# Weight tiles in three pools instead of one: where the operands of TensorE lie modulo 256 bytes

## The chip, the cores and the metric

The kernel runs on one core of a Trainium2 chip. The metric is the device time of one execution in microseconds (us), the median of several runs. "ns" is marked where it is meant.

## What is computed

One layer of a streaming encoder for two groups of tokens that share weights: 256 positions of a new stream and 32 of a running one, 288 together, with d_model 2048. Cut to what matters:

```python
xn = rmsnorm(x, norm_mix_pre)
u, z, xbc, dt = split(xn @ w_in)                  # 2048 -> 1024 + 2048 + 2560 + 32
mix = concat[pool_mixer(u), ssd_mixer(z, xbc, dt)] @ w_out      # 3072 -> 2048
x = x + rmsnorm(mix, norm_mix_post)
up = causal_dwconv(rmsnorm(x, norm_ffn_pre) @ w_up)             # 2048 -> 2 x 5632
x = x + rmsnorm((silu(gate) * value) @ w_down, norm_ffn_post)   # 5632 -> 2048
```

All is float32 in and out. The four large products are nearly all of the work.

## The kernel before

**Three products for one.** [...] A product of weights W and tokens A is then W_hi x A_hi + W_hi x A_lo + W_lo x A_hi. `mm3` issues these as three matmuls, on lines 144, 145 and 146; below they are called a triple. Each has 128 x 128 weights and 288 columns of tokens, and each loads its own weights first (on the page the loads are PEld). Tokens (`xn`, `mixs` and `mixp`, `hn`, `fa`: the inputs of the four large products) are tiles of 128 x 2 x 288 float32: the high half in front, the low half 1152 bytes behind it.

**Weights.** `fetch_w` (L119) loads `raw`, 8 tiles of contraction by 256 outputs, 8192 bytes per partition; `split_w` (L126) makes from each half of it a `whi` (ScalarE copies and rounds, L138) and a `wlo` (VectorE subtracts, L139), 4 contraction tiles by 256 outputs, 4096 bytes per partition each. All three kinds come from the pool `wpool`, four buffers of each tag (`hi`, `lo`, `raw`). `project` (L148) runs such a product: it walks over the contraction in chunks of 8 tiles (`ksplit`), for each chunk over the parts of 4, in each part over the two groups of 128 outputs, and in each of these over the 4 contraction tiles, one triple each, into one accumulator per 128 outputs. In the output projection the chunks are (8, 8), (16, 8), (0, 8): the SSD channels first (`mixs`), then the pooled channels `mixp0` to `mixp7`.

**Other users of TensorE.** The first stage (L361) multiplies the first columns of w_in by `xn` with weight tiles `w` of its own (both parts in one tile, in the pool `xin`), while the input still arrives: it holds 288 matmuls of 288 columns, hi x A_hi, hi x A_lo, lo x A_hi for each contraction tile and output. Its loads go to `raw` tiles, with one contraction tile into slots of the tags `hi` and `lo`. `state_mm` (L974) makes the new states, 512 columns at a time, with weights `bt_h` and `bt_l`. The last projection works with L1265 (high weights times both halves of 160 columns), L1266 (low weights, 288 columns) and L1288 (roles turned). L267 are 12 matmuls on a constant tile `busy` that run before the input is there.

**Addresses.** A pool's tiles stand behind each other in each partition, at multiples of 32 bytes, and pools stand in the order in which they are opened: `const`, `wpool`, `side`, `apool` (token tiles), `bpool`, then the stage's own. `side` holds four small tiles (`hp`, `eps_t`, `warm`, `rec`: 32 + 32 + 32 + 64 = 160 bytes). Weight and token tiles, and the steps between the slices of them that matmuls read (512 and 1024 bytes for weights), are such that each kind starts at one residue modulo 256, whichever buffer it is in (2304 bytes between token tiles is 9 x 256).

The order of instructions comes from a scheduler (`tc.high_priority`, `tc.issue_after` and `pin` bind it in places); the built programs have been laid beside each other for what the change does to it.

Of the kernel before, what the change touches and what calls it, by code (L numbers as in the profile page):

```python
# [8 lines left out]
F32 = mybir.dt.float32  # L9
F32R = mybir.dt.float32r  # L10
# [6 lines left out]
P = 128  # L17
# [8 lines left out]
HEADS = 32  # L26
# [16 lines left out]
NB = 768  # L43
# [15 lines left out]
def body(  # L59
# [23 lines left out]
    act, dve, pool, pe, sp = nc.scalar, nc.vector, nc.gpsimd, nc.tensor, nc.sync  # L83

    const = ctx.enter_context(tc.tile_pool(name="const", bufs=1))
    wpool = ctx.enter_context(tc.tile_pool(name="wpool", bufs=4))
    side = ctx.enter_context(tc.tile_pool(name="side", bufs=1))
    apool = ctx.enter_context(tc.tile_pool(name="apool", bufs=16))
    bpool = ctx.enter_context(tc.tile_pool(name="bpool", bufs=20))
    acc_ps = ctx.enter_context(tc.tile_pool(name="acc_ps", bufs=5, space=PSUM))  # L90
# [26 lines left out]
    pin = tc.keep_in_program_order  # L117

    def fetch_w(view, kb, nk, c0, nc_):  # L119
        raw = wpool.tile([P, nk, nc_], F32, tag="raw", name="raw")  # L120
        with tc.high_priority(offset=ahead[0]):
            group, c = divmod(c0, 2 * P)
            sp.dma_start(out=raw, in_=view[group, :, kb : kb + nk, c : c + nc_])
        return raw

    def split_w(raw, kb, nk, nc_, after=()):  # L126

        out = []
        step = min(nk, 1024 // nc_)
        for k in range(0, nk, step):  # L130
            n = min(step, nk - k)
            hi = wpool.tile([P, n, nc_], F32R, tag="hi", name="whi")
            lo = wpool.tile([P, n, nc_], F32R, tag="lo", name="wlo")
            with ExitStack() as order:
                order.enter_context(tc.high_priority(offset=ahead[0]))
                for ins in after:
                    order.enter_context(tc.issue_after(ins.ins))
                act.activation(hi, raw[:, k : k + n, :], AF.Copy)  # L138
                dve.tensor_tensor(lo, raw[:, k : k + n, :], hi.bitcast(F32), op=ALU.subtract)  # L139
            out.append([(kb + k + i, hi[:, i, :], lo[:, i, :]) for i in range(n)])  # L140
        return out
# [6 lines left out]
    def project(view, groups, acts, ksplit, before=None, done=None, spare=(), hold=(), behind=None, wait=(), tail=()):  # L148


        n_all = sum(-(-w // P) for _, w in groups)
        accs = [acc_ps.tile([P, NT], F32, tag="acc", name="acc") for m in range(n_all - len(spare))]
        accs.extend(spare)
        k_first, k_last = ksplit[0][0], ksplit[-1][0] + ksplit[-1][1] - 1
        after = before(*ksplit[0]) if before else None
        for i, (kb, n) in enumerate(ksplit):
            raws = [fetch_w(view, kb, n, c0, w) for c0, w in groups]
            nxt = None
            if before and i + 1 < len(ksplit):
                nxt = before(*ksplit[i + 1])  # L160
            m0 = 0
            for raw, (c0, w) in zip(raws, groups):
                parts = split_w(raw, kb, n, w, tuple(wait) + ((after or ()) if m0 else ()) + (hold if i else tail if m0 + w // P == n_all else ()))
                for q, part in enumerate(parts):
                    for m in range(w // P):
                        c = slice(m * P, (m + 1) * P)
                        with ExitStack() as order:
                            if behind and part[-1][0] == k_last and m0 + m > SUMS_AFTER:
                                order.enter_context(tc.issue_after(behind[-1].ins))
                            for k, hi, lo in part:  # L170
                                mm3(accs[m0 + m], hi[:, c], lo[:, c], acts[k], k == k_first, k == k_last)
                        if done and i + 1 == len(ksplit) and q + 1 == len(parts):
                            done(m0 + m, accs[m0 + m])
                m0 += w // P
            after = nxt
        return accs
# [33 lines left out]
    def first_load(i):  # L210

        kb, n = CHUNKS[i]
        raw = wpool.tile([P, n, NB], F32, tag="raw" if n > 1 else ("hi", "lo")[i % 2], name="raw")
        for j, c in enumerate((slice(0, NB),) if i else PIECES):
            pin((sp if i or j == 2 else act).dma_start(out=raw[:, :, c], in_=w_first[:, kb : kb + n, c]))
        raws.append(raw)

    input_load(0, 1)
    first_load(0)
    for i, (k0, k1) in enumerate(zip(INPUT[:-1], INPUT[1:])):  # L220
        input_load(k0, k1, sp if i else act)
        for j in range(2 * i + 1, 2 * i + 3):
            first_load(j)
    w_dt = xin.tile([P, KD, HEADS], F32, name="w_dt")
    pin(sp.dma_start(out=w_dt, in_=w_dt_in))
    first_load(9)
    cols = const.tile([P, sum(n for _, n in COLS)], F32, name="cols")
    pin(sp.dma_start(out=cols, in_=cols_in))
    hp = side.tile([HEADS, 3], F32, name="hp")
    pin(sp.dma_start(out=hp, in_=heads_in))  # L230
    col = {}
    for name, n in COLS:
# [2 lines left out]

    ones = const.tile([P, P], F32, name="ones")
    pool.memset(ones, 1.0)
    eps_t = side.tile([P, 1], F32, name="eps_t")
    pool.memset(eps_t, EPS)
    warm = side.tile([P, 1], F32, name="warm")  # L240
    pin(act.activation(warm, eps_t, AF.Copy))
    ident = const.tile([P, P], F32, name="ident")
    make_identity(nc, ident)
# [1 line left out]
    pool.affine_select(  # L245
        out=tri, in_=ones, pattern=[[1, P]], compare_op=ALU.is_ge, fill=0.0, base=0, channel_multiplier=-1
    )
    rec = side.tile([P, 16], F32, name="rec")
    for t in range(16):
        pool.memset(rec[:, t : t + 1], 1.0 / (t + 1))  # L250
    scan_one = const.tile([HEADS, NT], F32, name="scan_one")
# [572 lines left out]
    def pool_group(i):  # L824
        raw = fetch_w(w_pool, 2 * i, 2, 0, 256)
        wq = split_w(raw, 0, 2, 256)[0]
        for j in range(2):
            o = aux([P, NT], "acc_x") if j else acc_ps.tile([P, NT], F32, tag="acc", name="acc")
            c = slice(j * P, (j + 1) * P)
            for k, hi, lo in wq:  # L830
                mm3(o, hi[:, c], lo[:, c], uin[2 * i + k], k == 0, k == 1)
            a = op_.tile([P, 2, NT], F32R, name=f"mixp{2 * i + j}")
            split_from(a, o, p_scale[:, 2 * i + j : 2 * i + j + 1])
            mix[2 * i + j] = a
# [199 lines left out]
    late = []  # L1034
# [189 lines left out]
    K22 = [(0, 8), (8, 8), (16, 6)]  # L1224
    C1, C0 = slice(P, NT), slice(0, P)
    raws = [fetch_w(w_down[:, :, HALF:, :], kb, n, A * P, 256) for kb, n in K22]
    parts = []
    for (kb, n), raw in zip(K22, raws):
        for k in range(0, n, 4):
            m = min(4, n - k)  # L1230
            if len(parts) < 4:
                hi = wpool.tile([P, m, 256], F32R, tag="hi", name="whi")
                lo = wpool.tile([P, m, 256], F32R, tag="lo", name="wlo")
            else:
                rest = wpool.tile([P, 2, 4, 256], F32R, tag="raw", name="wlast")
                hi, lo = rest[:, 0, :m], rest[:, 1, :m]
            act.activation(hi, raw[:, k : k + m, :], AF.Copy)
            dve.tensor_tensor(lo, raw[:, k : k + m, :], hi.bitcast(F32), op=ALU.subtract)
            parts.append([(kb + k + i, hi[:, i, :], lo[:, i, :]) for i in range(m)])
    late_ = wpool.tile([P, 6 * P], F32, tag="raw", name="late")  # L1240
    ft.append(late_[:, : 4 * P])
    g_row = late_[:, 4 * P :]
    sp.dma_start(out=g_row, in_=norm_ffn_post[:, A * P :].broadcast_to([P, 2 * P]))
# [160 lines left out]
```

## Time and profile before

| | |
|---|---|
| median of 3 runs | 1322.2 us (1322.06 to 1324.41) |
| the profiled execution | 1322.35 us |
| its span, first to last instruction | 1320.6 us |
| TensorE busy | 1313.9 us, 99% |
| VectorE, ScalarE, GpSimd busy | 894.7, 672.5, 251.8 us |
| granted TensorE clock, mean | 1.000 |

A row of the timeline has start and duration in us, engine, line, operation, the tiles that it writes and reads, and its shape. Starts of consecutive matmuls tell how fast TensorE runs; a matmul's duration (some 0.29 us for 288 columns) is longer than the distance to the next one, since they overlap. In the windows a row has a stretch, its length, each engine's busy time with the number of its instructions that touch the stretch, the granted clock, and the busy share of the DMA engines. In the groups, "busy, mean ns of one | idle time before" follows the name and the count.

### The profile page before, as it was taken

Reading aid. Unit: us, or ns where it says so; the run is one execution under the profiler, and the core shown is the slowest. Engines: PE = TensorE matmul, PEld = TensorE weight load, DVE = VectorE, ACT = ScalarE, POOL = GpSimd, SP = SyncE. Lnnn points to the kernel's source line nnn. Section 1 sums busy time; section 2 is a strip of 40 time slices with the busy share of each in tenths; the row PEclk is TensorE's granted clock in tenths of the full one; section 3 lists DMA queues with packets and bytes.
Section 4 is the critical chain, followed back from the end, with each engine's and each line's share of the span. In section 5 each row is a group of like instructions: output and inputs, shape, how many; then the busy total and the mean of one; then the engine's idle time right before and its main releaser. Section 6 shows DMA issues by size and latency. Waiting matters only on the chain.

```text
span 1320.6 us, 25268 instructions
## 1 busy us (share of the span) xinstructions
PE 1313.9 (99%) x10043; PEld 1302.5 (99%) x10043; DVE 894.7 (68%) x1515; ACT 672.5 (51%) x1013; POOL 251.8 (19%) x399
## 2 busy tenths in 40 slices
PE   9999999999999999999999999999999999999998
PEld 9999999999999999999999999999999999999997
DVE  7998988879655588867766744336666666755454
ACT  7557767446543567544444433334444444444442
POOL 2342222222232221211211200001111111201110
PEclk9999999999999999999999999999999999999999
DMA  8578875445566478666445454455544554466763
GB/s 336 190 217 269 290 220 177 156 163 207 199 218 218 141 197 269 197 179 206 164 160 165 160 166 173 157 171 177 175 160 161 174 173 165 160 228 187 212 178 114
DMA packets 110038, 251.75 MB, mean 191 GB/s; under 512 B 64736, under 2 KB 73856, under 8 KB 87392
## 3 DMA queue, kind: packets, MB, share of 16 engines
q1 hardware_dynamic: 103424, 233.22, 54.7%
q0 software_dynamic: 5824, 16.13, 4.1%
q8 instruction: 78, 1.28, 0.4%
q10 hardware_dynamic: 672, 0.80, 0.2%
q14 instruction: 40, 0.33, 0.1%
HBM read 237.11 MB, written 13.00 MB: 189 GB/s over the span
## 4 chain that ended last, share of the span: by engine, by line
PE 96%; DMA 1%; DVE 1%; ACT 1%; issue 0%; SPq 0%; ACTq 0%
PE acc L145 30%; PE acc L144 30%; PE acc L146 30%; DMA raw<-in_w_first 1%; PE py L633 1%; PE acc L1265 0%; DVE w L300 0%; PE acc L1266 0%; PE acc_t L1288 0%; PE acc_x L145 0%; PE acc_x L144 0%; PE acc_x L146 0%; DVE sq L320 0%; PE py L635 0%; PE acc L361 0%; PE acc_x L361 0%
## 5 line engine op out<-in xcount | busy, mean ns | idle before, releaser
L139 DVE TENSOR_TENSOR wlo<-raw,whi 128x1024 fp32r<-128x1024 f32 (+1 forms) x396 | 472.9, 1196 | 311.9 <-ACT whi L138 310.3
L138 ACT ACTIVATE whi<-raw 128x1024 fp32r<-128x1024 f32 (+1 forms) x396 | 408.4, 1033 | 475.8 <-PE acc L145 394.1
L146 PE MATMUL acc<-hn,wlo 128*128 128x288 f32 x1376 | 404.5, 295 | 0.0
L145 PE MATMUL acc<-hn,whi 128*128 128x288 f32 x1376 | 403.6, 294 | 0.0
L144 PE MATMUL acc<-hn,whi 128*128 128x288 f32 x1376 | 402.9, 294 | 0.5 <-ACT hn L1041 0.4
L144 PEld LDWEIGHTS acc<-hn,whi 128*128 128x128 f32 x1376 | 258.8, 189 | 1.4 <-ACT hn L1041 0.8
L145 PEld LDWEIGHTS acc<-hn,whi 128*128 128x128 f32 x1376 | 258.5, 188 | 0.1
L146 PEld LDWEIGHTS acc<-hn,wlo 128*128 128x128 f32 x1376 | 258.3, 188 | 0.0
L146 PE MATMUL acc<-fa,wlo 128*128 128x288 f32 x660 | 194.6, 295 | 0.0
L145 PE MATMUL acc<-fa,whi 128*128 128x288 f32 x660 | 194.2, 294 | 0.0
L144 PE MATMUL acc<-fa,whi 128*128 128x288 f32 x660 | 194.0, 294 | 0.0
L146 PE MATMUL acc<-xn,wlo 128*128 128x288 f32 x608 | 179.5, 296 | 0.0
L144 PE MATMUL acc<-xn,whi 128*128 128x288 f32 x608 | 179.4, 295 | 0.0
L145 PE MATMUL acc<-xn,whi 128*128 128x288 f32 x608 | 178.9, 294 | 0.0
L144 PEld LDWEIGHTS acc<-fa,whi 128*128 128x128 f32 x660 | 124.5, 189 | 0.0
L145 PEld LDWEIGHTS acc<-fa,whi 128*128 128x128 f32 x660 | 124.1, 188 | 0.0
L146 PEld LDWEIGHTS acc<-fa,wlo 128*128 128x128 f32 x660 | 123.9, 188 | 0.0
L1091 POOL COPY fc_stage<-ebuf 128x4 f32<-128x4 f32 x88 | 26.9, 306 | 476.8 <-DVE ebuf L1090 455.4
L144 PEld LDWEIGHTS acc<-xn,whi 128*128 128x128 f32 x608 | 114.6, 189 | 0.7 <-issue 0.5
L145 PEld LDWEIGHTS acc<-xn,whi 128*128 128x128 f32 x608 | 114.3, 188 | 0.0
L146 PEld LDWEIGHTS acc<-xn,wlo 128*128 128x128 f32 x608 | 114.2, 188 | 0.1
L1086 POOL COPY ebuf<-cols 128x2 f32<-128x2 f32 x88 | 74.0, 842 | 108.7 <-DVE fc L1097 61.2
(338 smaller groups left out, 1800.1 us busy)
## 6 DMA issues: line engine op xcount, KB each, us to landing
raw<-in_w_up SPq DMA_DIRECT2D x80, 1024.0 KB, 5.1
raw<-in_w_in SPq DMA_DIRECT2D x38, 1024.0 KB, 5.2
raw<-in_w_down SPq DMA_DIRECT2D x32, 1024.0 KB, 5.0
raw<-in_w_out SPq DMA_DIRECT2D x24, 1024.0 KB, 5.0
raw<-in_w_down SPq DMA_DIRECT2D x16, 768.0 KB, 4.4
raw<-in_w_up SPq DMA_DIRECT2D x14, 512.0 KB, 4.2
gb<-g_d POOLq DMA_DIRECT2D x8, 832.0 KB, 6.3
raw<-in_w_first SPq DMA_DIRECT2D x5, 768.0 KB, 12.8
```

The source lines that it names most:

```text
L138: act.activation(hi, raw[:, k : k + n, :], AF.Copy)
L139: dve.tensor_tensor(lo, raw[:, k : k + n, :], hi.bitcast(F32), op=ALU.subtract)
L144: then(pe.matmul(out, wh, a[:, 0, :], start=start, stop=False))
L145: then(pe.matmul(out, wh, a[:, 1, :], start=False, stop=False))
L146: then(pe.matmul(out, wl, a[:, 0, :], start=False, stop=stop))
L633: ins = pe.matmul(y[c, 0:256], xw[:, 0, f_], m[:, h, 0:256], start=True, stop=False)
L1086: pool.tensor_copy(e[:, 258:260], hist_f[:, :, i])
L1091: pool.tensor_copy(fc_stage[:, :, :, i], e[:, 256:324].rearrange("p (s c) -> p s c", c=34)[:, :, 0:2])
```

## The change

`wpool` becomes three pools, opened in the order high, (side1), low, raw. `side1` holds only `rec`, 64 bytes; the other three small tiles go into `const`, which grows by 96. So the high parts move by 96 bytes, the low and raw ones by 160, and the token pool stays where it was. Sizes and numbers of buffers are the same. Start addresses modulo 256 in the two built programs:

| | before | after |
|---|---|---|
| `whi` | 64 | 160 |
| `wlo` | 64 | 224 |
| `raw` (and `wlast`, the last two parts of w_down) | 64 | 224 |
| first-stage `raw` of one contraction tile, in slots of `hi` and `lo` | 64 | 160, 224 |
| `xn`, `mixs`, `hn`, `fa`, `mixp4` to `7`, `du`, state tokens: high half | 224 | 224 |
| the same: low half | 96 | 96 |
| `mixp0` to `mixp3`: high half, low half | 96, 224 | 96, 224 |
| first-stage `w`, both parts | 160 | 160 |
| `bt_h`, `bt_l` | 96 | 96 |
| `busy` | 224 | 224 |
| `ones`, `ident`, `tri` and the other constants behind `cols` | | 32 or 96 more |

All 15064 instructions stand in the same order in both programs, on every engine and DMA queue, with the same operands' shapes and the same waits; only addresses (and the numbers in tile names) differ.

```diff
-    wpool = ctx.enter_context(tc.tile_pool(name="wpool", bufs=4))
-    side = ctx.enter_context(tc.tile_pool(name="side", bufs=1))
+    wpool = {"hi": ctx.enter_context(tc.tile_pool(name="whi", bufs=4))}
+    side1 = ctx.enter_context(tc.tile_pool(name="side1", bufs=1))
+    wpool["lo"] = ctx.enter_context(tc.tile_pool(name="wlo", bufs=4))
+    wpool["raw"] = ctx.enter_context(tc.tile_pool(name="wraw", bufs=4))
...
-        raw = wpool.tile([P, nk, nc_], F32, tag="raw", name="raw")
+        raw = wpool["raw"].tile([P, nk, nc_], F32, tag="raw", name="raw")
...
-            hi = wpool.tile([P, n, nc_], F32R, tag="hi", name="whi")
-            lo = wpool.tile([P, n, nc_], F32R, tag="lo", name="wlo")
+            hi = wpool["hi"].tile([P, n, nc_], F32R, tag="hi", name="whi")
+            lo = wpool["lo"].tile([P, n, nc_], F32R, tag="lo", name="wlo")
...
-    hp = side.tile([HEADS, 3], F32, name="hp")
+    hp = const.tile([HEADS, 3], F32, name="hp")
...
-    eps_t = side.tile([P, 1], F32, name="eps_t")
+    eps_t = const.tile([P, 1], F32, name="eps_t")
...
-    warm = side.tile([P, 1], F32, name="warm")
+    warm = const.tile([P, 1], F32, name="warm")
...
-    rec = side.tile([P, 16], F32, name="rec")
+    rec = side1.tile([P, 16], F32, name="rec")
```

The other places that take a tile from `wpool` (the first loads, the last projection) name the pool of their tag in the same way.

More of the change, by code (lines that the diff above doesn't have):

```diff
@@ L212, in first_load @@
         kb, n = CHUNKS[i]
-        raw = wpool.tile([P, n, NB], F32, tag="raw" if n > 1 else ("hi", "lo")[i % 2], name="raw")
+        tag = "raw" if n > 1 else ("hi", "lo")[i % 2]
+        raw = wpool[tag].tile([P, n, NB], F32, tag=tag, name="raw")
         for j, c in enumerate((slice(0, NB),) if i else PIECES):
@@ L1231, in body @@
             if len(parts) < 4:
-                hi = wpool.tile([P, m, 256], F32R, tag="hi", name="whi")
-                lo = wpool.tile([P, m, 256], F32R, tag="lo", name="wlo")
+                hi = wpool["hi"].tile([P, m, 256], F32R, tag="hi", name="whi")
+                lo = wpool["lo"].tile([P, m, 256], F32R, tag="lo", name="wlo")
             else:
-                rest = wpool.tile([P, 2, 4, 256], F32R, tag="raw", name="wlast")
+                rest = wpool["raw"].tile([P, 2, 4, 256], F32R, tag="raw", name="wlast")
                 hi, lo = rest[:, 0, :m], rest[:, 1, :m]
@@ L1239, in body @@
             parts.append([(kb + k + i, hi[:, i, :], lo[:, i, :]) for i in range(m)])
-    late_ = wpool.tile([P, 6 * P], F32, tag="raw", name="late")
+    late_ = wpool["raw"].tile([P, 6 * P], F32, tag="raw", name="late")
     ft.append(late_[:, : 4 * P])
```

## The prediction

> **What bounds the kernel now.** The page comes first: the shares of the engines, the chain that ended last, the splits, and a load of weights.
>
> ```profile
> span 1320.6 us, 25268 instructions
> ...
> PE 1313.9 (99%) x10043; PEld 1302.5 (99%) x10043; DVE 894.7 (68%) x1515; ACT 672.5 (51%) x1013; POOL 251.8 (19%) x399
> ...
> PE 96%; DMA 1%; DVE 1%; ACT 1%; issue 0%; SPq 0%; ACTq 0%
> ...
> L139 DVE TENSOR_TENSOR wlo<-raw,whi 128x1024 fp32r<-128x1024 f32 (+1 forms) x396 | 472.9, 1196 | 311.9 <-ACT whi L138 310.3
> L138 ACT ACTIVATE whi<-raw 128x1024 fp32r<-128x1024 f32 (+1 forms) x396 | 408.4, 1033 | 475.8 <-PE acc L145 394.1
> ...
> raw<-in_w_up SPq DMA_DIRECT2D x80, 1024.0 KB, 5.1
> ```
>
> TensorE is 96% of the chain, and it is never short of operands: the split on ScalarE (L138) idles 475.8 us, 394.1 of them because it waits for TensorE to give a weight buffer back. So the time is the number of matmuls times the distance between two of them. "Mean ns of one" doesn't give that distance: it includes a tail that the next matmul overlaps. The distance is read from start times.
>
> The program of the change has the same instructions in the same order on every engine, with the same waits; only addresses differ. The question is therefore whether a matmul's distance depends on where its operands lie. The next view is the timeline of the output projection.
>
> ```profile
> 404.12 0.29 PE L144 MATMUL acc<-mixs,whi 128*128 128x288 f32 x1
> 404.12 0.19 PEld L145 LDWEIGHTS acc<-mixs,whi 128*128 128x128 f32 x1
> ```
>
> The weights of the next matmul are loaded while this one streams its tokens. So I take as the pair that can disturb each other the tokens of one matmul and the weights of the next, and call D the start of those weights minus the start of those tokens, mod 256. With the table of addresses (weights at 64; tokens' high half at 224, low half at 96) a triple L144, L145, L146 has D = 96, 224, 96. The first four tiles of pooled channels (mixp0 to mixp3, halves swapped: 96 and 224) have 224, 96, 224. That is an experiment inside this trace: the same line, shape and buffers, first four tiles of the one kind, then four of the other, 4 tiles x 2 outputs x 3 = 24 matmuls each.
>
> ```profile
> 395.07 0.29 PE L144 MATMUL acc<-mixs,whi 128*128 128x288 f32 x1
> ...
> 404.51 0.30 PE L144 MATMUL acc<-mixp,whi 128*128 128x288 f32 x1
> ...
> 407.71 0.29 PE L144 MATMUL acc<-mixp,whi 128*128 128x288 f32 x1
> ...
> 410.86 0.29 PE L144 MATMUL acc<-mixs,whi 128*128 128x288 f32 x1
> ```
>
> mixp0 to 3 take 407.71 - 404.51 = 3.20 us, 133.3 ns a matmul and 400.0 a triple. mixp4 to 7 take 3.15 us: 131.25 and 393.75. The 72 mixs matmuls before them, with the addresses of mixp4 to 7, take 9.44 us: 131.1 and 393.3. Addresses matter, by 1.6%. In the long projections the triple is a little slower than mixs at the same addresses, shown by 36 triples of the up projection:
>
> ```profile
> 599.85 0.29 PE L144 MATMUL acc<-hn,whi 128*128 128x288 f32 x1
> ...
> 614.09 0.29 PE L144 MATMUL acc<-hn,whi 128*128 128x288 f32 x1
> ```
>
> 14.24 us / 108 = 131.85 ns, 395.6 a triple. Could other traffic be the cause? The windows say no (behind the engines' busy times a row has the granted clock, the share of DMA and GB/s): at full clock both, the fast half of mixp ran with the DMA engines 93% busy, the slow half with 42%.
>
> ```profile
> 404.51:407.71 3.20, 3.20 (x26) 3.20 (x25) 2.58 (x3) 1.06 (x1) 0.00 (x0) 1.00 0.42 166
> 407.71:410.86 3.15, 3.15 (x26) 3.15 (x25) 1.23 (x1) 1.87 (x3) 0.76 (x2) 1.00 0.93 312
> ```
>
> **Prices by distance.** Let c(D) be the distance to the next matmul. 2c(96) + c(224) = 395.6 and 2c(224) + c(96) = 400.0 give c(96) = 130.4 and c(224) = 134.8. The last projection confirms the first: its 288-column matmuls L1266 have D = 96 and the next start follows after 0.13 us.
>
> ```profile
> 1305.57 0.29 PE L1266 MATMUL acc<-fa,wlast 128*128 128x288 f32 x1
> 1305.70 0.31 PE L1265 MATMUL acc<-fa,wlast 128*128 128x320 f32 x1
> ```
>
> After the change the high weights lie at 160, the low ones at 224, the tokens where they were. A triple then has 160 - 224 = 192, 224 - 96 = 128, and 160 - 224 = 192: T = 2c(192) + c(128). For c(128) the nearest rows are the state matmuls L974, tokens at 224 and weights at 96:
>
> ```profile
> 371.29 0.39 PE L974 MATMUL pst<-xh,bt_h 128*128 128x512 f32 x1
> ...
> 372.68 0.39 PE L975 MATMUL pst<-xs,bt_s 96*128 96x512 f32 x1
> ```
>
> Six take 1.39 us, 231.7 ns for 512 columns; in proportion 288/512 x 231.7 = 130.3, an estimate. For c(192) there is the first stage (L361): its weights w stand at 160 in both parts, which gives 192, 64, 192.
>
> ```profile
> 19.82 3.36 PE L361 MATMUL acc<-xn,w 128*128 128x288 f32 x24
> 23.02 1.76 PE L361 MATMUL acc_x<-xn,w 128*128 128x288 f32 x12
> 24.62 3.36 PE L361 MATMUL acc<-xn,w 128*128 128x288 f32 x24
> ```
>
> From 19.82 to 24.62, 36 matmuls take 4.80 us: 133.3 ns, 2c(192) + c(64) = 400.0. One equation with two unknowns: c(64) from 130.4 (the lowest price seen) to 139.2 gives c(192) from 134.8 to 130.4. I take the first end, because each value then equals that of its measured neighbour, 64 that of 96 and 192 that of 224. T = 269.6 + 130.3 = 399.9.
>
> [...]
>
> **The sum**, against the profiled execution's 1322.35 us (0.15 above the median shown, 1.75 above its span). The triples are counted by the rows of line 144 (count, then the durations and the first and last start):
>
> ```profile
> L144 PE MATMUL acc<-hn,whi x1376: 292/293/512, 473.7 to 1171.0; 128*128 128x288 f32 x197
> L144 PE MATMUL acc<-fa,whi x660: 292/292/298, 753.7 to 1292.9; 128*128 128x288 f32 x165
> L144 PE MATMUL acc<-xn,whi x608: 291/293/401, 47.1 to 309.0; 128*128 128x288 f32 x152
> L144 PE MATMUL acc<-mixs,whi x256: 292/294/299, 311.0 to 454.6; 128*128 128x288 f32 x128
> L144 PE MATMUL acc<-mixp,whi x128: 292/294/298, 339.6 to 467.3; 128*128 128x288 f32 x128
> L144 PE MATMUL acc_x<-hn,whi x32: 292/297/299, 474.2 to 519.2; 128*128 128x288 f32 x32
> ```
>
> hn, fa and xn: 1376 + 32 + 660 + 608 = 2676 triples, each 399.9 - 395.6 = 4.3 ns more: +11.5 us. mixs and half of mixp: 256 + 64 = 320 triples, 399.9 - 393.4 = 6.5: +2.1 us. The other 64 of mixp get D = 64, 0, 64, between 391 and 396 by the prices above, against 400.0: -0.4 us. Sum +13.2, **1335.5 us**.
>
> What else moves costs nothing here. The splits read and write other addresses, and their price could move either way: L138 has 475.8 / 396 = 1.2 us of idle time for each instruction of 1.03 us, L139 311.9 / 396 = 0.8 beside 1.20, and both work up to four buffers ahead; only splits longer by more than that would reach TensorE. The weight loads land in 5.1 us a megabyte, which feeds 48 matmuls, 48 x 131.85 = 6.3 us; that 1.2 us is their cover. At the start, where TensorE waits for the first loads, 1% of DMA on the chain is 13 us; a tenth on that, gained or lost, is 1.3 us either way. The small tiles that go to the constants are read by no matmul of these stages.
>
> **The rivals.**
> - *Faster*: the same equation with the other end, c(192) = 130.4 and c(64) = 139.2. T = 391.1: 2676 x -4.5 = -12.0 us, 320 x -2.3 = -0.7, the 64 swapped triples 2 x 139.2 + 130.4 = 408.8, +0.6. Together **1310 us**. It decides as soon as c(192) is below (395.6 - 130.3) / 2 = 132.6. For it: no row separates 192 from 64. Against it: it needs a price at 64 that is above every one derived, beside 96 with the lowest.
> - *In between*: c(192) = c(64) = 133.3. T = 397.0: 2676 x 1.4 + 320 x 3.6 - 0.4 = +4.5 us, **1327 us**.
> - *Own weights*: a matmul disturbs itself where its weights and its tokens have one address mod 256. The low weights now have the address of the tokens' high half, so each L146 pays. With the largest step between two prices seen, 4.4 ns, on top: 2996 x 4.4 = +13.2, **1349 us**. The only matmuls of this shape with one address are the warm-up ones, L267, whose weights and tokens are the same tile; the windows at the start (TensorE's busy time alone, then clock, DMA share and GB/s) have them in their first row.
>
> ```profile
> 1.70:3.90 2.20, 2.20 (x11) 1.00 0.86 251
> 4.40:5.20 0.80, 0.80 (x4) 1.00 1.08 389
> ```
>
>   Eleven in 2.20 us are 200 ns or more each, which would be +68 x 2996 = +200 us at the least. But the first L361 behind them, with other addresses, are no quicker (4 in 0.80 us) where later ones take 133.3 ns, so it is the start that is slow, and I leave that end out. [...]
> - *Nothing*: what differs between the stages is their order of work and not the address; **1322 us**. The mixp halves speak against it.
>
> **How the numbers follow.** Forecast 0.46, in between 0.11, own weights 0.05: slower 0.62. Faster 0.32. Nothing 0.06. A measurement of this kernel can tell about 0.2% (2.6 us) from no change, which is 0.3 ns a matmul. The range takes in the faster rival with 2 us for the start and for a c(128) that is only an estimate, and on the other side leaves out the own-weights case: 1308 to 1346.
>
> **What would show it.** In the changed profile the span of 36 triples in the up projection should be 36 x 399.9 ns = 14.40 us instead of 14.24; 14.08 is the faster rival. The first stage should keep its 4.80 us for 36 matmuls, and mixp0 to 3 should fall below 3.20 us. L138 should idle longer, since TensorE gives buffers back later. The prediction is wrong if the three matmuls of a triple don't add up by pairs as I assume, for instance because the rhythm of several triples counts and not each pair: mixs and hn, with the same D, already differ by 2 ns a triple, and that much I can't explain.

## The result, and the profile after

The changed kernel takes **1315.57 us** (median of 4 runs, 1314.58 to 1315.95), the kernel before 1322.4 us beside it (1322.06 to 1324.41): ratio 0.9944, 95% interval 0.9927 to 0.9961. The forecast was slower, 1335.5 us; it is faster, by 7 us.

The page of the changed kernel: span, busy shares, chain by engine, and from the groups the two splits (now L140 and L141) and the triple of the up projection (now L146, L147, L148). Behind a group's name stand the number, busy us and mean ns of one, then the idle time before and what ended it.

```profile
span 1313.5 us, 25268 instructions
...
PE 1306.5 (99%) x10043; PEld 1295.5 (99%) x10043; DVE 894.9 (68%) x1515; ACT 671.7 (51%) x1013; POOL 250.6 (19%) x399
...
PE 94%; DMA 2%; issue 1%; DVE 1%; ACT 0%; POOL 0%; SPq 0%; POOLq 0%; ACTq 0%
...
L141 DVE TENSOR_TENSOR wlo<-raw,whi 128x1024 fp32r<-128x1024 f32 (+1 forms) x396 | 473.6, 1198 | 305.9 <-ACT whi L140 304.4
L140 ACT ACTIVATE whi<-raw 128x1024 fp32r<-128x1024 f32 (+1 forms) x396 | 408.1, 1032 | 466.9 <-PE acc L147 370.5
L146 PE MATMUL acc<-hn,whi 128*128 128x288 f32 x1376 | 405.5, 296 | 0.8 <-ACT hn L1044 0.4
L147 PE MATMUL acc<-hn,whi 128*128 128x288 f32 x1376 | 401.9, 293 | 0.0
L148 PE MATMUL acc<-hn,wlo 128*128 128x288 f32 x1376 | 398.1, 290 | 0.0
```

The same triple on the page of the kernel before, costliest line first:

```profile
L146 PE MATMUL acc<-hn,wlo 128*128 128x288 f32 x1376 | 404.5, 295 | 0.0
L145 PE MATMUL acc<-hn,whi 128*128 128x288 f32 x1376 | 403.6, 294 | 0.0
L144 PE MATMUL acc<-hn,whi 128*128 128x288 f32 x1376 | 402.9, 294 | 0.5 <-ACT hn L1041 0.4
```

The 7.1 us that the span lost are TensorE's: its busy time fell by 7.4. ScalarE's split takes as long as before (408.1 us, 408.4 before); its idle time fell from 475.8 to 466.9 us and VectorE's from 311.9 to 305.9, each by about what the span lost, where the prediction had ScalarE's grow. The three lines of a triple, equal within a nanosecond before, now differ, 296, 293 and 290 ns. Start to start, averaged over every row of those lines, the distances behind L146, L147 and L148 are 135.0, 131.1 and 128.4 ns; before they were 132.5, 131.5 and 132.6 behind L144, L145 and L146. Summed, the triples lost 6.5 us, the first stage 0.4 and the last projection 0.2.

The timeline of the changed kernel, TensorE alone, at the places that the prediction named: first stage, the two halves of mixp, and 36 triples of the up projection (a row with x24 joins 24 matmuls, so it starts where the first does).

```profile
19.61 3.36 PE L364 MATMUL acc<-xn,w 128*128 128x288 f32 x24
22.81 1.76 PE L364 MATMUL acc_x<-xn,w 128*128 128x288 f32 x12
24.41 3.36 PE L364 MATMUL acc<-xn,w 128*128 128x288 f32 x24
...
402.16 0.29 PE L146 MATMUL acc<-mixp,whi 128*128 128x288 f32 x1
...
405.32 0.29 PE L146 MATMUL acc<-mixp,whi 128*128 128x288 f32 x1
...
408.46 0.30 PE L146 MATMUL acc<-mixs,whi 128*128 128x288 f32 x1
...
599.98 0.30 PE L146 MATMUL acc<-hn,whi 128*128 128x288 f32 x1
...
614.14 0.30 PE L146 MATMUL acc<-hn,whi 128*128 128x288 f32 x1
```

The first stage keeps its 4.80 us for 36 matmuls. mixp0 to 3 take 3.16 us instead of 3.20, mixp4 to 7 3.14 instead of 3.15. The 36 triples take 14.16 us, 393.3 ns each, where the forecast had 14.40 and the kernel before 14.24.

### The profile page after: what moved, and what is told of

Its sections match the earlier page's. It is cut to its first block, busy times and chain, and to the rows that moved or that the text cites. A ratio compares the mean times of both kernels' runs of the same rounds, so it can differ in the third digit from the quotient of the medians.

```text
span 1313.5 us, 25268 instructions
## 1 busy us (share of the span) xinstructions
PE 1306.5 (99%) x10043; PEld 1295.5 (99%) x10043; DVE 894.9 (68%) x1515; ACT 671.7 (51%) x1013; POOL 250.6 (19%) x399
## 4 chain that ended last, share of the span: by engine, by line
PE 94%; DMA 2%; issue 1%; DVE 1%; ACT 0%; POOL 0%; SPq 0%; POOLq 0%; ACTq 0%
PE acc L146 30%; PE acc L147 30%; PE acc L148 29%; DMA raw<-in_w_first 1%; PE py L636 1%; PE acc L1268 0%; DVE w L303 0%; PE acc L1269 0%; DMA mg<-in_x_g 0%; PE acc_t L1291 0%; DVE sq L323 0%; PE py L638 0%; PE acc L364 0%; PE acc_x L364 0%; PE acc_x L146 0%
## 5 line engine op out<-in xcount | busy, mean ns | idle before, releaser
L141 DVE TENSOR_TENSOR wlo<-raw,whi 128x1024 fp32r<-128x1024 f32 (+1 forms) x396 | 473.6, 1198 | 305.9 <-ACT whi L140 304.4
L140 ACT ACTIVATE whi<-raw 128x1024 fp32r<-128x1024 f32 (+1 forms) x396 | 408.1, 1032 | 466.9 <-PE acc L147 370.5
L146 PE MATMUL acc<-hn,whi 128*128 128x288 f32 x1376 | 405.5, 296 | 0.8 <-ACT hn L1044 0.4
L147 PE MATMUL acc<-hn,whi 128*128 128x288 f32 x1376 | 401.9, 293 | 0.0
L148 PE MATMUL acc<-hn,wlo 128*128 128x288 f32 x1376 | 398.1, 290 | 0.0
L146 PEld LDWEIGHTS acc<-hn,whi 128*128 128x128 f32 x1376 | 257.7, 188 | 1.7 <-ACT hn L1044 0.8
L147 PEld LDWEIGHTS acc<-hn,whi 128*128 128x128 f32 x1376 | 258.1, 188 | 0.1
L148 PEld LDWEIGHTS acc<-hn,wlo 128*128 128x128 f32 x1376 | 258.1, 188 | 0.0
L146 PE MATMUL acc<-fa,whi 128*128 128x288 f32 x660 | 195.4, 296 | 0.0
L147 PE MATMUL acc<-fa,whi 128*128 128x288 f32 x660 | 193.4, 293 | 0.0
L148 PE MATMUL acc<-fa,wlo 128*128 128x288 f32 x660 | 191.4, 290 | 0.0
L146 PE MATMUL acc<-xn,whi 128*128 128x288 f32 x608 | 179.3, 295 | 0.0
L147 PE MATMUL acc<-xn,whi 128*128 128x288 f32 x608 | 178.5, 294 | 0.0
L148 PE MATMUL acc<-xn,wlo 128*128 128x288 f32 x608 | 177.5, 292 | 0.0
L146 PEld LDWEIGHTS acc<-fa,whi 128*128 128x128 f32 x660 | 123.9, 188 | 0.0
L147 PEld LDWEIGHTS acc<-fa,whi 128*128 128x128 f32 x660 | 123.9, 188 | 0.0
L148 PEld LDWEIGHTS acc<-fa,wlo 128*128 128x128 f32 x660 | 123.9, 188 | 0.0
L146 PEld LDWEIGHTS acc<-xn,whi 128*128 128x128 f32 x608 | 114.2, 188 | 0.7 <-issue 0.5
L148 PEld LDWEIGHTS acc<-xn,wlo 128*128 128x128 f32 x608 | 114.1, 188 | 0.1
L147 PEld LDWEIGHTS acc<-xn,whi 128*128 128x128 f32 x608 | 114.0, 188 | 0.0
```

The lines of the kernel that those rows point to most:

```text
L146: then(pe.matmul(out, wh, a[:, 0, :], start=start, stop=False))
L147: then(pe.matmul(out, wh, a[:, 1, :], start=False, stop=False))
L148: then(pe.matmul(out, wl, a[:, 0, :], start=False, stop=stop))
```

## The experiments

Four theories stood against each other. **Prices by pair**, the prediction's: each neighbouring pair of matmuls has a price set by two addresses, with other values than I chose. **Rhythm**: a triple settles into a repeating pattern that high weights, low weights and tokens set together. **64 bytes**: what counts is a distance of 64 between the parts. **Loads**: the gain comes from splits and loads at their new places. An address is given below as its residue modulo 256; tokens are at 224 (high half) and 96 (low half). Each whole kernel ran four times or more, each small kernel once; the granted clock is 0.999 or 1.000 in every profile.

The whole kernels, with the 36 triples read at the same place of each. A ratio is to the kernel before as it ran beside that kernel (1322.35 to 1323.1 us), not to the first row. The raw tiles stand at the residue of the low weights, except in "raw alone".

| kernel | high, low weights | ns a triple | median us | ratio to before, 95% |
|---|---|---|---|---|
| before | 64, 64 | 395.6 | 1322.4 | 1 |
| the change | 160, 224 | 393.3 | 1315.57 | 0.9944 (0.9927 to 0.9961) |
| high part alone | 160, 64 | 400.0 | 1335.35 | 1.0091 (1.0074 to 1.0108) |
| low part alone | 64, 224 | 400.0 | 1334.88 | 1.0090 (1.0075 to 1.0105) |
| all at 160 | 160, 160 | 400.0 | 1335.11 | 1.0091 (1.0076 to 1.0107) |
| raw alone (at 224) | 64, 64 | 395.6 | 1322.20 | 0.9999 (0.9990 to 1.0009) |
| swapped | 224, 160 | 396.7 | 1323.62 | 1.0010 (1.0000 to 1.0019) |
| distance 96 | 224, 64 | 393.3 | 1315.45 | 0.9948 (0.9931 to 0.9964) |

**A map of residues.** A small kernel leaves the layer out and runs blocks of 30 triples, one block for each pair of residues, from one weight tile and one token tile:

```
+    for h in range(8):
+        for l in range(8):
+            accs.append(block(f"h{L[h]}l{L[l]}", ((h, 0), (h, NT), (l, 0))))
+    for w in range(8):
+        accs.append(block(f"only{L[w]}", ((w, 0),), 90))
```

> This kernel leaves the whole layer out (its outputs are zeros) and only times triples: 64 blocks of 30 triples, high weights at 8 residues mod 256 (a to h: 0, 32, ... 224) by low weights at 8 residues, tokens fixed at 224 and 96 as in the layer; then 8 blocks of 90 matmuls with one weight tile. Pairs theory (only the tokens of one matmul and the weights of the next count): the time of a triple is 2c(high + 32) + c(low + 160), so a row of the map is another row plus a constant; high 64 with low 64 takes 395.6 ns, 160 with 224 393.3 ns, 160 with 160 400.0 ns, and (64, 224) and (160, 64) add up to 788.9. Rhythm theory (the delays of one matmul shift the next, and the whole triple settles into a rhythm): rows aren't parallel, and a triple takes one of few lengths, such as 393.3, 395.6 and 400.0, most of them equal. Theory that addresses don't count: 72 equal blocks.

Its timeline, TensorE: in a block's name the letters behind h and l are the residues of the high and the low weights, a for 0 to h for 224 in steps of 32. A block's length is the next row's start minus its own.

```profile
223.90 12.03 PE L83 MATMUL hclc<-tok,wgt 128*128 128x288 f32 x90
235.77 12.16 PE L83 MATMUL hcld<-tok,wgt 128*128 128x288 f32 x90
...
283.57 12.16 PE L83 MATMUL hclh<-tok,wgt 128*128 128x288 f32 x90
295.57 12.06 PE L83 MATMUL hdla<-tok,wgt 128*128 128x288 f32 x90
...
510.07 12.15 PE L83 MATMUL hflc<-tok,wgt 128*128 128x288 f32 x90
522.06 12.16 PE L83 MATMUL hfld<-tok,wgt 128*128 128x288 f32 x90
...
546.06 12.16 PE L83 MATMUL hflf<-tok,wgt 128*128 128x288 f32 x90
558.06 12.16 PE L83 MATMUL hflg<-tok,wgt 128*128 128x288 f32 x90
...
570.06 11.96 PE L83 MATMUL hflh<-tok,wgt 128*128 128x288 f32 x90
581.86 12.16 PE L83 MATMUL hgla<-tok,wgt 128*128 128x288 f32 x90
```

(64, 64) takes 11.87 us, 395.7 ns a triple, and (160, 224) 11.80 us, 393.3: the kernel before and the change, with nothing of the layer around them. (64, 224) takes 12.00 and (160, 64) 11.99, 400 each, and (160, 160), the residues of the first stage, 12.00. Now the test of prices by pair. In a triple the high weights stand beside tokens, and so do the low ones; by pairs the length is a term of the high residue plus one of the low residue, and (64, 64) + (160, 224) must equal (64, 224) + (160, 64). They are 789.0 and 799.7. No choice of prices mends that. The whole kernels say the same further down: 395.6 + 393.3 against 400.0 + 400.0. Every one of the 64 pairs lies between 393 and 400 ns, thirteen of them within 0.6 ns of the shortest.

**One part of the change alone**, in the whole kernel. Pads of unread bytes move single pools, and the token pool stays put. The high part, then the low part with the raw one, then all three at 160:

```
 high alone
-    side1 = ctx.enter_context(tc.tile_pool(name="side1", bufs=1))
+    pad_b = ctx.enter_context(tc.tile_pool(name="pad_b", bufs=1))
+    side1 = pad_b
+    pad_b.tile([P, 24], F32, name="gap_b")
+    pad_d.tile([P, 40], F32, name="gap_d")
 low alone
+    pad_a.tile([P, 40], F32, name="gap_a")
+    pad_b.tile([P, 24], F32, name="gap_b")
 all at 160 (side1 behind raw, nothing between the three)
-    side1 = ctx.enter_context(tc.tile_pool(name="side1", bufs=1))
+    side1 = pad_d
```

> Only the high parts move (64 to 160), low parts and raw stay at 64. Pairs theory: D is 192, 224, 192 instead of 96, 224, 96; this and lo_only together change the time by what the whole change did, -6.9 us. If a step of 64 between high weights and tokens is what helps, all of it comes here: about 1315.5 us, 393.3 ns a triple. If the offset of the low parts is what helps: no gain here, 1322 us or more, 395.6 to 400 ns.

> Only the low parts (and raw, which TensorE does not read) move, 64 to 224; the high parts stay at 64. Pairs theory: D is 96, 128, 96 instead of 96, 224, 96; with the old price of 96 a triple takes 260.8 + c(128), about 391 ns, 1309 us. If a step of 64 between high weights and tokens is what helps: no change, 1322 us. If low weights at the tokens' own residue help: about 1315 us.

> High, low and raw all at 160: the addresses that the first stage has already. Pairs theory: 400.0 ns a triple as in the first stage, +13 us, 1335 us. Theory that only the token's distance to the high weights counts: like the change, 1315.6 us, 393.3 ns. Rhythm theory: one of the known lengths, 400.0 if the first stage's rhythm comes from its addresses alone.

The same 36 triples of the up projection, from the timelines of the three kernels in that order (the triple's first line is L150, L150 and L147 there).

```profile
599.92 0.29 PE L150 MATMUL acc<-hn,whi 128*128 128x288 f32 x1
...
614.32 0.29 PE L150 MATMUL acc<-hn,whi 128*128 128x288 f32 x1
```

```profile
599.93 0.30 PE L150 MATMUL acc<-hn,whi 128*128 128x288 f32 x1
...
614.33 0.30 PE L150 MATMUL acc<-hn,whi 128*128 128x288 f32 x1
```

```profile
600.10 0.30 PE L147 MATMUL acc<-hn,whi 128*128 128x288 f32 x1
...
614.50 0.30 PE L147 MATMUL acc<-hn,whi 128*128 128x288 f32 x1
```

All three take 14.40 us, 400.0 a triple, and the kernels some 12 us more than the kernel before beside them. Prices by pair had the two halves of the change add up to its -6.9 us; they add up to +24. Each half alone costs about what the forecast gave to the whole, and both together gain 7. The map had all three lengths. "All at 160" is the prediction's case in pure form: its 400.0 is the first stage's 400.0, and it is what the change would have cost if the low weights had gone to 160 as well.

**Raw alone.** High and low weights stay at 64; the raw tiles go to 224, the small tiles as in the change.

```
+    side1 = pad_c
+    pad_a.tile([P, 40], F32, name="gap_a")
+    pad_c.tile([P, 24], F32, name="gap_c")
```

> Only raw (and the constants) move, as in the change; high and low parts stay at 64. Rhythm theory and pairs theory: as before, 1322 us, 395.6 ns a triple. Theory that the gain comes from the splits or the loads (they read and write raw): 1315.5 us.

```profile
600.09 0.29 PE L150 MATMUL acc<-hn,whi 128*128 128x288 f32 x1
...
614.33 0.29 PE L150 MATMUL acc<-hn,whi 128*128 128x288 f32 x1
```

14.24 us for the 36, as before, and a ratio of 0.9999. So the loads, and the raw tiles that the splits read, have no visible part in the gain. The theory of the loads falls.

**Order, start and common shift.** The layer is left out again. Blocks of 20 triples: another order of the three matmuls (q), every second triple reversed (s), eight different lead-in matmuls ("kicks") ahead of the four pairs above (k), and all three operands shifted together (t).

```
+            k_ = ps.tile([P, NT], F32, tag="kick", name="kick")
+            pin(pe.matmul(k_[:, :kick], wgt[:, 0:P], tok[:, 0:kick], start=True, stop=True))
...
+            accs.append(block(f"k{L[h]}{L[l]}{L[k]}", ((h, 0), (h, NT), (l, 0)), kick=104 + 8 * k))
...
+            accs.append(block(f"t{L[h]}{L[l]}{L[k]}", ((h + k, 8 * k), (h + k, NT + 8 * k), (l + k, 8 * k))))
```

> Leaves the whole layer out, as map does, and times blocks of 20 triples. First 64 pairs of residues in the order high x A_hi, low x A_hi, high x A_lo; then 64 pairs with every second triple in the reverse order; then four pairs of residues, (64, 64), (160, 224), (160, 64), (64, 224), each entered eight times behind one matmul of another width; then the same four pairs with weights and tokens all moved on together by 0 to 224 bytes. Rhythm theory: lengths again lie between 393.3 and 400.0 in steps of 3.3 ns, the order of the three changes which pairs are short; (64, 64) shows 395.6 behind some widths and 393.3 behind others, since the long stages and the output projection had these two at the same addresses; moving all together by 64 changes nothing. Theory that each matmul has a price of its own by its addresses: the other order gives the same map, and the entry changes nothing.

Behind a lead-in the first triples are slower: at (160, 224) a block takes 7.91 to 7.94 us from its start to the next lead-in's, and 7.87 or 7.88 to the next block's where no lead-in stands between (the t blocks). So there a block's length is read start to start over its last 36 matmuls, in the trace's nanoseconds; a row's own length holds the slow start and a tail besides. Two of the eight blocks at (64, 224), behind a lead-in of 112 and of 128 columns:

```profile
1230.01 8.22 PE L86 MATMUL kchb<-tok,wgt 128*128 128x288 f32 x60
...
1246.23 8.09 PE L86 MATMUL kchd<-tok,wgt 128*128 128x288 f32 x60
```

0.13 us over 20 triples is 6.5 ns a triple: the same addresses run at 400.0 or at 393.3, by how they were entered. At this pair four of the eight entries give 400.0, one 396.7 and three 393.3. The blocks share two accumulators, and two places can't give three lengths, so the place of the result alone is not the cause. (160, 224) gives 393.3 from all eight, (64, 64) 395.6 and (160, 64) 400.0 from all eight. I had expected (64, 64) to show two lengths here, and it didn't. Shifting all operands together changes nothing at (160, 224), (64, 64) and (160, 64), and (64, 224), entered without a lead-in there, stays at one value, 396.7. No fixed price of an address can give two lengths for one set of addresses; of the four theories, what remains is a rhythm.

The order of the three counts too. With the low weights in the middle (q) the block at (160, 224), the change's pair, is slow:

```profile
383.85 8.16 PE L86 MATMUL qfh<-tok,wgt 128*128 128x288 f32 x60
391.85 8.16 PE L86 MATMUL qga<-tok,wgt 128*128 128x288 f32 x60
```

8.00 us are 400.0 ns a triple. With every second triple reversed (s) that pair takes 396.7. Both sets of 64 reach from 393.3 to 403.3, past the 400.0 that I had expected as the upper end, and other pairs are the short ones. So the gain of the change belongs to the kernel's order of the three, as far as one block of each pair and order can tell.

**Swapped**: high weights at 224, low at 160, still 64 bytes apart, and 393.3 in the map.

```
+    side1 = pad_b
+    pad_a.tile([P, 16], F32, name="gap_a")
+    pad_b.tile([P, 32], F32, name="gap_b")
+    pad_d.tile([P, 16], F32, name="gap_d")
```

> High parts at 224, low ones at 160: the residues of the change exchanged, so the high weights stand at the very residue of the tokens' high half. Rhythm theory with the map (224, 160: 393.3): 1315.5 us, like the change. Theory that high weights must stand 64 from the tokens: 1322 us or more. Pairs theory from the records before: high weights at 224 give D = 0, 64, 0, which no row excludes.

```profile
599.75 0.30 PE L152 MATMUL acc<-hn,whi 128*128 128x288 f32 x1
...
614.03 0.30 PE L152 MATMUL acc<-hn,whi 128*128 128x288 f32 x1
```

14.28 us, 396.7 a triple, and 1323.62 us. I had expected the gain of the change, from the single block of the map, and that was wrong. The next kernel asks why.

**More entries, and another distance of the token halves.** The layer is left out. Eleven pairs with eight lead-ins each, then 448 blocks of 16 triples with the low token half moved by 32 to 224 bytes:

```
+    for h, l in ((0, 7), (1, 3), (2, 4), (3, 3), (4, 1), (4, 2), (4, 7), (5, 1), (6, 1), (7, 2), (7, 5)):
+        for k in range(8):
+            accs.append(block(f"k{L[h]}{L[l]}{L[k]}", ((h, 0), (h, NT), (l, 0)), kick=104 + 8 * k))
...
+                accs.append(block(f"d{L[d]}{L[h]}{L[l]}", ((h, 0), (h, NT + 8 * d), (l, 0)), 16))
```

> Leaves the whole layer out, as map does. First the other eleven pairs of residues that map had near 393.3 ns, each entered eight times behind one matmul of another width, in the kernel's order of the three. Rhythm theory: some reach 393.3 from every start (like 160, 224 in map2), the others 396.7 or 400.0 from some; (224, 160), which took 396.9 ns in the kernel swapped, must be one of these. Then all 64 pairs with the tokens' low half at seven other distances from the high half (160 to 352, mod 256, instead of 128). If 393.3 is a floor of this stream of matmuls, no block is shorter; if it only comes from the distance of the token halves, some are.

Two of the eight blocks at (224, 160), and the block that took longest of the 448, with the one behind it:

```profile
658.31 8.16 PE L86 MATMUL khfb<-tok,wgt 128*128 128x288 f32 x60
...
666.36 8.09 PE L86 MATMUL khfc<-tok,wgt 128*128 128x288 f32 x60
...
2776.60 6.67 PE L86 MATMUL dgae<-tok,wgt 128*128 128x288 f32 x48
2783.11 6.57 PE L86 MATMUL dgaf<-tok,wgt 128*128 128x288 f32 x48
```

(224, 160) has both rhythms: 8.09 us for 393.3, 8.16 for 396.7, and seven entries of eight give the slow one. The whole kernel runs at that length, and so "swapped" gained nothing. Four pairs gave 393.3 from all eight entries, (224, 64) among them; (224, 96), which was as short in the map, was not entered again. Of the 448 blocks the longest took 6.51 us, some 407 ns a triple. The shortest take 6.29 us, 393.1 as far as 0.01 us can tell, so no block settled clearly below 393.3, and the change runs at it.

**Distance 96**: (224, 64), one of those four. Neither the two kinds of weights nor the high weights and the tokens stand 64 bytes apart here.

```
+    side1 = pad_b
+    pad_a.tile([P, 16], F32, name="gap_a")
+    pad_b.tile([P, 8], F32, name="gap_b")
+    pad_d.tile([P, 40], F32, name="gap_d")
```

> High parts at 224, low ones at 64: another pair that took 393.3 ns from all eight starts in map3, with no distance of 64 between high weights and tokens or low parts. Rhythm theory: 393.3 ns a triple in the long stages and 1315.5 us, like the change. Theory that the 64 bytes of the change are what helps: 1322 us or more.

```profile
599.82 0.29 PE L152 MATMUL acc<-hn,whi 128*128 128x288 f32 x1
...
613.98 0.29 PE L152 MATMUL acc<-hn,whi 128*128 128x288 f32 x1
```

14.16 us and 1315.45: the same gain as the change. The 64 bytes are not what counts: with them "swapped" gained nothing, and without them this kernel gains all of it. It doesn't beat the change; both are at the shortest length found.

**The 2 ns between mixs and hn.** The layer is left out. Blocks of 40 triples at (64, 64) and (160, 224), each behind 4 to 11 triples with the token halves exchanged, as mixp0 to 3 stand ahead of others in the kernel:

```
+            block(f"w{L[h]}{L[l]}{L[k]}", ((h, NT), (h, 0), (l, NT)), 4 + k)
+            accs.append(block(f"k{L[h]}{L[l]}{L[k]}", ((h, 0), (h, NT), (l, 0)), 40))
```

> Leaves the whole layer out. Blocks of 40 triples at (64, 64) and at (160, 224), each behind 4 to 11 triples whose token halves are exchanged (the first takes the other's address), as mixp0 to mixp3 stand in the output projection. Rhythm theory: at (64, 64) some blocks settle at 393.3 ns, as mixs does there, and others at 395.6; at (160, 224) all at 393.3. Theory that the output projection is faster for another reason: 395.6 in all blocks at (64, 64).

The first two blocks at (64, 64) (kcca, kccb), then the first at (160, 224), each with the row behind it:

```profile
10.73 15.90 PE L86 MATMUL kcca<-tok,wgt 128*128 128x288 f32 x120
26.47 2.17 PE L86 MATMUL wccb<-tok,wgt 128*128 128x288 f32 x15
28.47 15.99 PE L86 MATMUL kccb<-tok,wgt 128*128 128x288 f32 x120
44.30 2.56 PE L86 MATMUL wccc<-tok,wgt 128*128 128x288 f32 x18
...
160.96 15.89 PE L86 MATMUL kfha<-tok,wgt 128*128 128x288 f32 x120
176.69 2.14 PE L86 MATMUL wfhb<-tok,wgt 128*128 128x288 f32 x15
```

15.74 us and 15.83: (64, 64) settles at 393.3 or at 395.6, four of eight each. They differ in what ran ahead: for the first two, four or five exchanged triples and the blocks before those. (160, 224) settles at 393.3 in all eight. So (64, 64) too has a fast rhythm. In the kernel before, most of mixs had fallen into it (152 of 212 stretches of three triples), and hn never had (none of 1315).

The slow rhythm itself stands in the trace of the kernel before, at the start of the 36 triples that the prediction read:

```profile
599.85 0.29 PE L144 MATMUL acc<-hn,whi 128*128 128x288 f32 x1
599.98 0.29 PE L145 MATMUL acc<-hn,whi 128*128 128x288 f32 x1
...
600.63 0.30 PE L144 MATMUL acc<-hn,whi 128*128 128x288 f32 x1
600.77 0.30 PE L145 MATMUL acc<-hn,whi 128*128 128x288 f32 x1
```

From L144 to L145 it is 130 or 131 ns in two triples and 135 in the third, and so through the 36: the three take some 391, 391 and 404 ns. All have the same residues; 395.6 is the mean of a pattern three triples long.

## Why the prediction was wrong, point by point

- **TensorE bounds the kernel, and its distance between matmuls is the time**: right. 6.5 of the 7.1 us of span are the triples.
- **Addresses move that distance**: right. Whole kernels that differ in addresses alone lie between 1315.5 and 1335.4 us. No run shows where inside TensorE that time is lost.
- **Prices by distance**: this step failed. It took one price c(D) for each pair of tokens and next weights, and T = 2c(192) + c(128) came to 399.9 with c(192) = 134.8, where a triple measured 393.3. First, the first stage's 2c(192) + c(64) = 400.0 was split wrongly: with c(128) = 130.3 the measured T asks for c(192) = 131.5 and c(64) = 137.0. The first stage is slow because its low weights stand at 160 too; with the high ones at 160, low ones at 160 give 400.0 and at 224 393.3. Second, and deeper, no such prices fit the runs. Moving the low weights from 64 to 224 puts c(128) in place of c(224), and the whole kernels show it at +4.4 ns with the high weights at 64 and at -6.7 with them at 160. In the changed kernel the distances behind L146 and L148 have the same D = 192 and are 135.0 and 128.4 ns; in the kernel before the distance behind L144 alone is 130 and 135. Nor does c(96) = 130.4 hold alone: 90 matmuls with one weight tile at 64 and tokens at 224 take 133.3 ns each in the map. The 130.3 for c(128) was no clean reading either, since the tokens' low half at 96 gives the six L974 rows D = 128, 0, 128 by turns. What the traces show is a rhythm of whole triples, and terms taken from other rhythms missed this one: 399.9 ns against 393.3.
- **Counts**: right. 2676 triples x (393.3 - 395.6) = -6.2 us, 64 of mixp x (395 - 400) = -0.3: -6.5 with the measured T. (The 395 of mixp0 to 3 lies in the 391 to 396 foretold.) The forecast's +13.2 came from its 399.9 alone.
- **Splits, loads and start cost nothing**: right for loads and raw tiles (0.9999 with the raw tiles moved alone). First stage: 4.80 us for 36 as foretold, with 0.4 us gained over its whole length.
- **The rivals**: the faster one came nearer (1310) but not by its mechanism. It has the same additive prices, and its T of 391.1 is shorter than any length that a block or stage settled at. The time lies in the stated range only because the range reached down to this rival, and that is luck. Own weights: wrong; the low weights have the residue of their own tokens, and the distance behind those matmuls is the shortest of the three (128.4 ns, beside 135.0 and 131.1). Nothing: wrong.
- **The doubt**: the last paragraph's reserve, that the rhythm of several triples counts, is what happened. The 2 ns between mixs and hn was the evidence, already in the trace; I named it and gave it no share of the chances.

Left open: what inside TensorE sets the rhythm. That the weight load of one matmul disturbs the token reads of another was the prediction's assumption, and no run shows it. Nor was the token pool moved, or the order of the three changed, in the whole kernel.

## What to carry to other kernels

Where TensorE is the bound, measure start to start, and vary the residues of weights and tokens together: here each half of a good move alone cost 0.9%, and both gained 0.6%. A small kernel of blocks in the kernel's own order finds good pairs in one run; prefer a pair that gives its length from several entries, and then measure the whole kernel. Eight entries are no proof: (64, 64) gave 395.6 from all eight lead-ins, and 393.3 in half of the blocks of the last experiment. Two stages with equal addresses and unequal lengths in a trace are a warning that a price per pair may be the wrong model.

## What the runs showed of the hardware

- The length of three 288-column matmuls depends on where weights and tokens lie modulo 256 bytes, 393.3 to 400.0 ns with this kernel's token halves and order, up to 403.3 in other orders of the three, and up to some 407 with other distances between the halves; shifting everything together, in steps of 32 bytes, gave one length for all eight shifts of each pair tried. The map's blocks and the whole kernels, with the same residues at other places, gave the same lengths: 395.7 and 395.6 ns at (64, 64), 393.3 in both at (160, 224).
- The settled lengths were mostly 393.3, 396.7 and 400.0, steps of 3.3 ns; at (64, 64), as before the change, 395.6, the mean of a pattern three triples long.
- With the same addresses TensorE can stay in either of two lengths, by what ran ahead: blocks of 40 triples at (64, 64) kept 393.3 or 395.6 to their end, and in the kernel before none of the up projection ran in the faster (0 of 1315 stretches of three triples).
